# Splitting h's combinations in the up turns, and preparing the weights of down's first two turns together

## The chip, the core and the metric

The kernel runs on one core of a Trainium2 chip. Its time is the device time in microseconds; the kernel before has a median of 2336.82 us over 3 runs (2336.71 to 2340.5). The engines are PE (TensorE, the matmuls), DVE (VectorE), ACT (ScalarE), POOL (GpSimd, which also issues some transfers) and SP (SyncE, which only issues transfers).

## The reference

One layer of a streaming encoder: a combined input projection, a pooling mixer and a differential attention side by side, an output projection, a SwiGLU feed-forward and a final norm. All is float32. The change lies in the feed-forward alone:

```python
def _swiglu(h, g_ffn, w_gate, w_up, w_down):
    n = _rmsnorm(h, g_ffn)
    return h + (jax.nn.silu(n @ w_gate) * (n @ w_up)) @ w_down
```

D_MODEL is 2048 and D_FF 5632. 576 tokens (16 meta, 512 prompt, 64 sample) go through it together.

## The kernel before

**Arithmetic.** Each large product is made by Strassen and Winograd's scheme: a 2x2 block product with seven block products instead of eight, on combinations of the operands' blocks. Every operand is split in a high part (rounded to fp32r by an ACT copy) and a low part (operand minus high, on DVE), and a block product is the sum of high·high, high·low and low·high, three matmuls (L804 to L806) of 128x128 by 128x288. The class `Seven` makes one such turn: `load` fetches four raw weight blocks (L783, on SP), `prep(i)` makes the combinations (L789 to L793, DVE) and their split (L833/L834 in gate/up, L1030/L1031 in down: ACT then DVE), `product(i)` issues the matmuls of product i into one of three PSUM banks and calls the evacuation. Products 3, 4, 5 and 6 reuse the banks of products 0, 1, 2 and 4, so product 6 can start only when the evacuation of product 4 has read its bank. `run` walks over all (turn, product) steps and issues `prep` three products ahead of `product`.

**Stages.** Input projection, attention, output projection, then gate/up from about 850 us to 1776 us, down to about 2300 us, and the final norm with its output.

**Gate/up.** `seq` holds 44 turns: for f = 0 to 21 a gate turn (PSUM banks `mm`) and an up turn (banks `pj`), 168 matmuls each. The evacuations i = 0 to 6 of a turn are made in `inner`: i=0 an ACT copy (L860), i=1 (L862), i=2 (L865, the tile `t5`), i=3 (L867), i=4 (L869), i=5 (L871), i=6 (L873) on DVE. After the last, POOL multiplies by the gate (L875, L876), and in `up_evac` makes four combinations of the seven blocks of h (L904 to L907), in the tile `ho` of 128 x 7 x 288, and stores it to DRAM as `hd[f]` (L908, 1008 KB, issued by POOL). The engines' queues are in order: what stands behind a waiting instruction waits too.

**Down.** 40 turns n, by rounds r and output blocks m. The turns of the first round contract over 2, 2, 3, 3, 4, 4, 5, 5 values of f, later ones over 5. `h_operand` (L1015) loads a piece of `hd[f]` (288 KB for q < 3, 144 KB for q = 3) into a staging tile `sx`, and `h_split` (L952 ACT, L953 DVE) splits it into a slot: 20 full slots (16 of them, `act`, free when gate/up's operands are done) and 7 half slots. The pieces q = 0 to 2 of f = 0 and 1 are loaded (L967) and split already during the last up turn. Evacuations are an ACT copy (L1044) in the first round, later a DVE addition (L1050) or a POOL transfer that accumulates (L1048).

Of the kernel before, what the change touches and what calls it, by code (L numbers as in the profile page):

```python
# [19 lines left out]
P = 128  # L20
# [30 lines left out]
def hymba_step(  # L51
# [717 lines left out]
    class Seven:  # L769


        def __init__(self, src, j0, nj, c0, raws, tmp, splits, xs_, psum, evac):
            self.src = src.rearrange("(j two p) n -> p two j n", p=P, two=2)[:, :, j0:j0 + nj, c0:c0 + 2 * P]
# [75 lines left out]
    hd = [dram.tile([P, 7, TN], F32, name=f"hd{j}") for j in range(FT // 2)]  # L849
# [46 lines left out]
    def up_evac(f):  # L896
        def evac(s, i):
            if i == 0:
                s.ho = fw.tile([P, 7, TN], F32, name="ho")
            h = s.ho  # L900
            inner(s, i, (h[:, 0], h[:, 6], h[:, 3], h[:, 5], h[:, 3:6:2]), blocks(gates[f]))
            if i == 6:
                tt = nc.gpsimd.tensor_tensor
                tt(h[:, 2], h[:, 6], h[:, 0], op=ALU.subtract)  # L904
                tt(h[:, 1], h[:, 5], h[:, 2], op=ALU.subtract)
                tt(h[:, 4], h[:, 5], h[:, 6], op=ALU.subtract)
                tt(h[:, 6], h[:, 3], h[:, 1], op=ALU.subtract)  # L907
                nc.gpsimd.dma_start(out=hd[f], in_=h)  # L908
        return evac
# [30 lines left out]
    FULL, HALF, ACTS = 20, 7, KT  # L940
    hc, nfull, queue = {}, [0], [(f, q) for f in range(NFP) for q in range(4)]

    def full_slot(shape, name, dtype=F32R):
        k = nfull[0]
        nfull[0] += 1
        if k % FULL < ACTS:
            return act.tile(shape, dtype, name=name, tag="act")
        return dw.tile(shape, dtype, name=name, tag="hc", bufs=FULL - ACTS)
# [6 lines left out]
    EARLY = 2  # L955

    def early_operands(n, i):
        if n < len(seq) - 1 or i not in (1, 2, 3):
            return
        if i == 1:  # L960
            for f in range(EARLY):
                for q in range(3):
                    hc[f, q] = full_slot([P, 2, 2, TN], f"hc{q}")
        for f in range(EARLY):
            r = fw.tile([P, 8, P], F32, name="raw", bufs=5)
            s = r.rearrange("p k c -> p (k c)")[:, :2 * TN].rearrange("p (q t) -> p q t", q=2)
            nc.sync.dma_start(out=s, in_=hd[f][:, 2 * i - 2:2 * i])  # L967
            h_split(f, i - 1, s)
# [16 lines left out]
    first_use = {f: min(n for n, (m, f0, f1) in enumerate(turns) if f0 <= f < f1) for f in range(NFP)}  # L985

# [16 lines left out]
    rw.tile([P, 2, TN], F32, name="sx", tag="sx", bufs=3)  # L1003
    yt += [rw.tile([P, 4, TN], F32, name=f"y{m}") for m in range(4, NR)]
    def h_free(f, q, n, i):

        if q == 3:
            return f < HALF or (last_use[f - HALF], 6) <= (n, i)
        k = 3 * f + q - FULL
        return k < 0 or (last_use[k // 3], (1, 4, 5)[k % 3]) <= (n, i)  # L1010

    def h_operand(f, q):
        w = 2 if q < 3 else 1
        s = rw.tile([P, 2, TN], F32, name="sx", tag="sx", bufs=3)
# [86 lines left out]
    seq = []  # L1101
    for n, (m, j0, j1) in enumerate(turns):
        psum = (lambda: banks(pz, "mm", "mm")) if n % 2 == 0 else (lambda: banks(pj, "pj", "pj"))
        seq.append(Seven(w_down[0], j0, j1 - j0, m * 2 * P,
                         lambda n, nj=j1 - j0: rw.tile([P, DJ, P], F32, name="raw", tag="raw", bufs=6)[:, :nj],
                         lambda nj=j1 - j0: rw.tile([P, DJ, P], F32, name="wt", tag="wt", bufs=1)[:, :nj],
                         split_block, lambda i, j, j0=j0: hc[j0 + j, i // 2][:, i % 2], psum, down_evac(n, m)))
    seq[0].load()
    while queue[0][0] < turns[0][2]:
        fq = queue.pop(0)  # L1110
        if fq not in hc:
            h_operand(*fq)
# [4 lines left out]
    run(seq, hooks, order=(1, 0, 2, 4, 3, 5, 6))  # L1117
# [60 lines left out]
```

## Time and profile before

| | us |
|---|---|
| median of 3 runs | 2336.82 |
| span of the profiled execution | 2332.2 |
| PE busy | 2257.0 (97%) |
| DVE busy | 1883.4 (81%) |
| ACT busy | 1149.1 (49%) |
| POOL busy | 507.5 (22%) |

The profiled execution has a span of 2332.2 us, 4.6 us less than the median of the runs. Times within it count from its start. A row of the timeline reads: start, duration, engine, line, operation, output <- input, shapes, count, and in brackets the idle time ahead of it with what ended it. A row of the table by windows reads: window, length, then busy time and number of instructions of PE, PE's weight loads, DVE, ACT and POOL, the granted clock of PE, the busy share of the DMA engines and the rate in GB/s.

### The profile page before, as it was taken

What the parts mean: (1) busy time and instruction counts of PE and PEld (TensorE: products, weight loads), DVE (VectorE), ACT (ScalarE), POOL (GpSimd) and SP (SyncE); (2) the same over time, 40 slices, a digit from 0 to 9 for tenths busy, and PEclk for the clock granted to TensorE, in tenths of its full rate; (3) what the DMA queues carried; (4) which work ended last, traced back from release to release, by engine and by line L of the source; (5) the groups of instructions that cost most, each with busy time, mean ns of one, the idle gap of its engine ahead of it and who ended that gap; (6) DMA issues with size and microseconds to landing.
All of it is one profiled execution on the core that took longest, in us unless ns stands there. A gap on an engine that the chain in (4) does not pass through costs nothing.

```text
span 2332.2 us, 43585 instructions
## 1 busy us (share of the span) xinstructions
PE 2257.0 (97%) x16815; PEld 2231.5 (96%) x16815; DVE 1883.4 (81%) x3474; ACT 1149.1 (49%) x2423; POOL 507.5 (22%) x461
## 2 busy tenths in 40 slices
PE   7999999999999899999999999999997999999995
PEld 6999999999999899999999999999997999999994
DVE  6888888875477888888888888888887778888887
ACT  5666666643244544444444444444445555555544
POOL 1100000001225132322322323323231012211222
PEclk9999999999999999999999999999999999999998
DMA  6433333223234333433434333343344479867643
GB/s 174 113 89 102 90 97 106 72 73 93 79 88 123 106 114 109 136 109 118 125 111 122 115 126 118 110 134 117 104 138 150 135 185 202 207 168 179 162 96 112
DMA packets 426370, 286.00 MB, mean 123 GB/s; under 512 B 13075, under 2 KB 405453, under 8 KB 426164
## 3 DMA queue, kind: packets, MB, share of 16 engines
q1 hardware_dynamic: 403184, 226.50, 33.8%
q0 software_dynamic: 22144, 55.30, 9.6%
q8 instruction: 132, 2.16, 0.4%
q10 hardware_dynamic: 836, 1.43, 0.2%
q14 instruction: 74, 0.61, 0.1%
HBM read 233.65 MB, written 40.35 MB: 117 GB/s over the span
## 4 chain that ended last, share of the span: by engine, by line
PE 88%; DVE 4%; issue 3%; DMA 3%; ACT 1%; POOL 0%; SPq 0%; DVEq 0%; ACTq 0%; POOLq 0%
PE pj L804 10%; PE pj L806 10%; PE mm L804 10%; PE pj L805 10%; PE mm L806 10%; PE mm L805 10%; PE pj L112 6%; PE pj L114 6%; PE pj L113 6%; PE mm L113 3%; PE mm L112 3%; PE mm L114 3%; DMA sx<-hd 1%; DVE ws L1031 1%; PE S L426 1%
## 5 line engine op out<-in xcount | busy, mean ns | idle before, releaser
L834 DVE TENSOR_TENSOR ws<-raw,ws 128x512 fp32r<-128x512 f32 x430 | 384.1, 909 | 74.1 <-ACT ws L833 71.6
L833 ACT ACTIVATE ws<-raw 128x512 fp32r<-128x512 f32 x430 | 264.6, 630 | 345.7 <-PE pj L806 122.2
L804 PE MATMUL mm<-xc,ws 128*128 128x288 f32 x1232 | 365.3, 297 | 7.7 <-ACT ws L833 7.5
L804 PE MATMUL pj<-xc,ws 128*128 128x288 f32 x1232 | 365.1, 296 | 3.1 <-ACT ws L833 3.1
L805 PE MATMUL mm<-xc,ws 128*128 128x288 f32 x1232 | 363.4, 295 | 0.0
L805 PE MATMUL pj<-xc,ws 128*128 128x288 f32 x1232 | 363.2, 295 | 0.0
L806 PE MATMUL pj<-xc,ws 128*128 128x288 f32 x1232 | 361.7, 294 | 0.8 <-DVE ws L834 0.8
L806 PE MATMUL mm<-xc,ws 128*128 128x288 f32 x1232 | 361.6, 293 | 0.2 <-DVE ws L834 0.2
L112 PE MATMUL pj<-x,ws 128*128 128x296 f32 (+1 forms) x1024 | 317.9, 311 | 9.1 <-ACT x L106 8.5
L113 PE MATMUL pj<-x,ws 128*128 128x296 f32 (+1 forms) x1024 | 306.8, 300 | 0.0
L114 PE MATMUL pj<-x,ws 128*128 128x296 f32 (+1 forms) x1024 | 305.3, 298 | 0.0
L804 PEld LDWEIGHTS mm<-xc,ws 128*128 128x128 f32 x1232 | 231.8, 188 | 8.5 <-ACT ws L833 8.0
L804 PEld LDWEIGHTS pj<-xc,ws 128*128 128x128 f32 x1232 | 232.0, 188 | 3.3 <-ACT ws L833 3.3
L806 PEld LDWEIGHTS pj<-xc,ws 128*128 128x128 f32 x1232 | 233.2, 189 | 1.1 <-DVE ws L834 1.1
L806 PEld LDWEIGHTS mm<-xc,ws 128*128 128x128 f32 x1232 | 233.2, 189 | 0.4 <-DVE ws L834 0.4
L805 PEld LDWEIGHTS mm<-xc,ws 128*128 128x128 f32 x1232 | 232.9, 189 | 0.1
L805 PEld LDWEIGHTS pj<-xc,ws 128*128 128x128 f32 x1232 | 232.9, 189 | 0.0
L137 ACT ACTIVATE ws<-wraw,vcols 128x128 fp32r<-128x128 f32 x512 | 169.5, 392 | 106.8 <-PE pj L114 87.7
L112 PEld LDWEIGHTS pj<-x,ws 128*128 128x128 f32 x1024 | 193.1, 189 | 14.3 <-ACT x L106 9.2
L1030 ACT ACTIVATE ws<-raw 128x640 fp32r<-128x640 f32 (+3 forms) x200 | 133.5, 673 | 130.3 <-DVE raw L791 44.4
L113 PEld LDWEIGHTS pj<-x,ws 128*128 128x128 f32 x1024 | 193.7, 189 | 0.4
L114 PEld LDWEIGHTS pj<-x,ws 128*128 128x128 f32 x1024 | 192.8, 188 | 0.0
(338 smaller groups left out, 5772.0 us busy)
## 6 DMA issues: line engine op xcount, KB each, us to landing
raw<-in_w_up_dram SPq DMA_DIRECT2D x88, 512.0 KB, 3.8
raw<-in_w_gate_dram SPq DMA_DIRECT2D x84, 512.0 KB, 3.8
raw<-in_w_down_dram SPq DMA_DIRECT2D x112, 320.0 KB, 4.4
wraw<-in_w_in_dram SPq DMA_DIRECT2D x64, 512.0 KB, 4.1
hd<-ho POOLq DMA_DIRECT2D x22, 1008.0 KB, 5.7
sx<-hd SPq DMA_DIRECT2D x60, 288.0 KB, 3.7
wraw<-in_w_out_dram SPq DMA_DIRECT2D x32, 512.0 KB, 3.9
y<-ev POOLq DMA_DIRECT2D x60, 144.0 KB, 3.7
```

Source lines behind the costliest of these rows:

```text
L112: nc.tensor.matmul(ps, lhsT=w(0), rhs=x(0), start=first, stop=False)
L113: nc.tensor.matmul(ps, lhsT=w(0), rhs=x(1), start=False, stop=False)
L114: return nc.tensor.matmul(ps, lhsT=w(1), rhs=x(0), start=False, stop=last)
L137: nc.scalar.activation(ws[:, 0, k, :], r[:, k, :], AF.Copy, scale=g)
L426: nc.tensor.matmul(ps, lhsT=self.q[:, 2 + m, qs], rhs=kt[:, m, c0:c1], start=False, stop=True)
L804: nc.tensor.matmul(ps, lhsT=w(0), rhs=x(0), start=first and j == 0, stop=False, skip_group_check=True)
L805: nc.tensor.matmul(ps, lhsT=w(0), rhs=x(1), start=False, stop=False, skip_group_check=True)
L806: mm = nc.tensor.matmul(ps, lhsT=w(1), rhs=x(0), start=False, stop=j == self.nj - 1, skip_group_check=True)
L833: nc.scalar.activation(ws[:, 0], src[:, k:k + WK], AF.Copy)
L834: nc.vector.tensor_tensor(ws[:, 1], src[:, k:k + WK], ws.bitcast(F32)[:, 0], op=ALU.subtract)
L1030: nc.scalar.activation(ws[:, 0], src, AF.Copy)
L1031: nc.vector.tensor_tensor(ws[:, 1], src, ws.bitcast(F32)[:, 0], op=ALU.subtract)
```

## The change

**Storing.** For f < 21, `up_evac` splits the seven blocks of h on the spot. ACT copies blocks 0 to 3 to a tile `hi` in fp32r (128x1152), DVE subtracts it from them in place, POOL stores `hi`; the same for blocks 4 to 6 (128x864); then POOL stores the low parts. `hi` has the tag `xlast`, of which there is one buffer. `hd[f]` gets a further axis of two, high and low. f = 21 is stored unsplit.

**Loading.** `h_operand` loads high and low straight into the slot, 576 KB (q < 3) or 288 KB, with no staging tile and no split. For f = 21 the piece comes block by block through `ev` tiles and is split as before. The slots are 16 `act` and 5 `hc`, given out by when they come free; the half slots are 5 and 3.

**Weights of down's turns 0 and 1.** A `Seven` with two output blocks at once loads, combines and splits them during the last up turn into seven `we` tiles in act slots. The first 14 products of down alternate between the two turns. The rest of down goes as before, with turn 2's raw weights loaded ahead of the loop, and h pieces of f >= 3 issued behind them.

```diff
-    hd = [dram.tile([P, 7, TN], F32, name=f"hd{j}") for j in range(FT // 2)]
+    hd = [dram.tile([P, 7, 2 if j < FT // 2 - 1 else 1, TN], F32, name=f"hd{j}") for j in range(FT // 2)]
...
                 tt(h[:, 6], h[:, 3], h[:, 1], op=ALU.subtract)
-                nc.gpsimd.dma_start(out=hd[f], in_=h)
+                if f == FT // 2 - 1:
+                    nc.gpsimd.dma_start(out=hd[f][:, :, 0], in_=h)
+                    return
+                for q, w in ((0, 4), (4, 3)):
+                    hi = fs.tile([P, 4, TN], F32R, name="hi", tag="xlast")
+                    nc.scalar.activation(hi[:, :w], h[:, q:q + w], AF.Copy)
+                    nc.vector.tensor_tensor(h[:, q:q + w], h[:, q:q + w], hi.bitcast(F32)[:, :w], op=ALU.subtract)
+                    nc.gpsimd.dma_start(out=hd[f][:, q:q + w, 0], in_=hi.bitcast(F32)[:, :w])
+                nc.gpsimd.dma_start(out=hd[f][:, :, 1], in_=h)
...
-    def h_split(f, q, s):
-        t, w = hc[f, q], 2 if q < 3 else 1
-        nc.scalar.activation(t[:, 0:w, 0], s[:, :w], AF.Copy)
-        nc.vector.tensor_tensor(t[:, 0:w, 1], s[:, :w], t.bitcast(F32)[:, 0:w, 0], op=ALU.subtract)
...
+    def h_operand(f, q):
+        w, t = 2 if q < 3 else 1, h_slot(f, q)
+        if f < NFP - 1:
+            nc.sync.dma_start(out=t.bitcast(F32), in_=hd[f][:, 2 * q:2 * q + w])
+            return
+        for i in range(w):
+            s = dw.tile([P, TN], F32, name="ev", tag="ev", bufs=4)
+            nc.sync.dma_start(out=s, in_=hd[f][:, 2 * q + i, 0])
+            nc.scalar.activation(t[:, i, 0], s, AF.Copy)
+            nc.vector.tensor_tensor(t[:, i, 1], s, t.bitcast(F32)[:, i, 0], op=ALU.subtract)
...
+    def split_early(src):
+        step = ORDER.index((0, 1, 2, 4, 3, 5, 6)[len(early.w)])
+        n = EARLY * turns[0][2]
+        t = full_slot([P, 1152], "we", (EARLY - 1, step))[:, :2 * n * P].rearrange("p (i j c) -> p i j c", i=2, j=n)
+        nc.scalar.activation(t[:, 0], src, AF.Copy)
+        nc.vector.tensor_tensor(t[:, 1], src, t.bitcast(F32)[:, 0], op=ALU.subtract)
+        return t
...
+        if i == 3:
+            early.load()
+        if i in (0, 1, 3):
+            for f in range(2):
+                h_operand(f, (0, 1, None, 2)[i])
+        for p in ((), (), (), (0, 1), (2, 4), (3, 5, 6), ())[i]:
+            early.prep(p)
...
         if queue and h_free(*queue[0], n, i):
-            h_operand(*queue.pop(0))
+            later = n < EARLY and queue[0][0] >= 3
+            with tc.issue_after(down[EARLY].loaded.ins) if later else ExitStack():
+                h_operand(*queue.pop(0))
...
+        if n < EARLY:
+            down[n].w = {i: lambda k, j, t=t, n=n: t[:, k, 2 * n + j, :] for i, t in early.w.items()}
...
-    run(seq, hooks, order=(1, 0, 2, 4, 3, 5, 6))
+    run(down, hooks, done=7 * EARLY, order=ORDER)
```

The numbers of lines move by 3 to 5 around this place: L833/L834 become L837/L838, the evacuations L860 to L873 become L864 to L877 (i=4 is L873 now), POOL's L904 to L907 become L908 to L911; the new lines are L917 (ACT copy to `hi`), L918 (DVE subtraction), L919 (POOL stores of `hi`), L920 (store of the low parts), L988 (h loads) and L1002/L1003 (split of the early weights).

How the instructions stand in DVE's queue during a gate turn, from behind L873 of the up turn that precedes it; before (`g` is the gate turn's result, `ws` and `wt` are weights):

```order
L834 TENSOR_TENSOR ws<-raw,ws 128x512 x4
L862 TENSOR_TENSOR pu<-mm,pu 128x288
L834 TENSOR_TENSOR ws<-wt,ws 128x512 x2
L789 TENSOR_TENSOR wt<-raw 128x1024
L865 TENSOR_TENSOR t_14935<-mm,pu 128x288
L834 TENSOR_TENSOR ws<-raw,ws 128x512
L790 TENSOR_TENSOR raw<-raw 128x1024
L834 TENSOR_TENSOR ws<-raw,ws 128x512
L867 TENSOR_TENSOR g<-mm,rp 128x288
L834 TENSOR_TENSOR ws<-raw,ws 128x512 x2
L791 TENSOR_TENSOR raw<-wt,raw 128x1024
L869 TENSOR_TENSOR g<-mm,t_14935 128x288
```

With the change, from the evacuation i=1 on (two splits, the first L918 of 128x1152 and two more splits stand between L877 and it):

```order
L866 TENSOR_TENSOR pu<-mm,pu 128x288
L838 TENSOR_TENSOR ws<-wt,ws 128x512
L918 TENSOR_TENSOR ho<-ho,hi 128x864
L838 TENSOR_TENSOR ws<-wt,ws 128x512
L869 TENSOR_TENSOR t_15015<-mm,pu 128x288
L793 TENSOR_TENSOR wt<-raw 128x1024
L838 TENSOR_TENSOR ws<-raw,ws 128x512 x2
L794 TENSOR_TENSOR raw<-raw 128x1024
L871 TENSOR_TENSOR g<-mm,rp 128x288
L838 TENSOR_TENSOR ws<-raw,ws 128x512 x2
L795 TENSOR_TENSOR raw<-wt,raw 128x1024
L873 TENSOR_TENSOR g<-mm,t_15015 128x288
```

The second subtraction L918 stands ahead of the evacuations i=2 to i=4 of the gate turn (L869, L871, L873).

ACT's queue at the same place, with the change; before, the rows are the same without the two L917:

```order
L837 ACTIVATE ws<-raw 128x512 x2
L917 ACTIVATE hi<-ho 128x1152
L864 ACTIVATE pu<-mm 128x288
L837 ACTIVATE ws<-raw 128x512 x2
L837 ACTIVATE ws<-wt 128x512
L917 ACTIVATE hi<-ho 128x864
L837 ACTIVATE ws<-wt 128x512
L837 ACTIVATE ws<-raw 128x512 x6
L837 ACTIVATE ws<-wt 128x512 x2
```

And POOL's, one up turn's end:

```order
L879 TENSOR_TENSOR ho<-ho,g 128x288
L908 TENSOR_TENSOR ho<-ho 128x288
L880 TENSOR_TENSOR ho<-ho,g 128x2x288
L909 TENSOR_TENSOR ho<-ho 128x288
L910 TENSOR_TENSOR ho<-ho 128x288
L911 TENSOR_TENSOR ho<-ho 128x288
L919 DMA hd_9867<-hi 128x4x288
L919 DMA hd_9867<-hi 128x3x288
L920 DMA hd_9867<-ho 896x1x288
```

The second `hi` of ACT uses the buffer that the first L919 reads; the three stores take the place of one.

SP's queue where down's turn 3 gets its raw weights (128x3x128, the second group of four); f is `hd_9862` plus its number; `sx` is the staging tile. Before:

```order
L1015 DMA sx<-hd_9864 128x576 x3
L783 DMA raw<-in_w_down_dram 128x2x128 x2
L1015 DMA sx<-hd_9864 128x288
L783 DMA raw<-in_w_down_dram 128x3x128
L1015 DMA sx<-hd_9865 128x576 x2
L783 DMA raw<-in_w_down_dram 128x3x128
L1015 DMA sx<-hd_9865 128x576
L1015 DMA sx<-hd_9865 128x288
L1015 DMA sx<-hd_9866 128x576
L783 DMA raw<-in_w_down_dram 128x3x128
L1015 DMA sx<-hd_9866 128x576
L783 DMA raw<-in_w_down_dram 128x3x128
```

With the change:

```order
L988 DMA hh<-hd_9869 128x576
L786 DMA raw<-in_w_down_dram 128x3x128 x4
L988 DMA hc_20901<-hd_9865 128x1152
L988 DMA hc_20910<-hd_9865 128x1152
L988 DMA hc_20919<-hd_9865 128x1152
L988 DMA hh<-hd_9865 128x576
L988 DMA hc_20940<-hd_9866 128x1152
L988 DMA hc_20949<-hd_9866 128x1152
L988 DMA hc_20958<-hd_9866 128x1152
L988 DMA hh<-hd_9866 128x576
L988 DMA hc_20986<-hd_9867 128x1152
L786 DMA raw<-in_w_down_dram 128x3x128 x4
```

Before, the raw weights of turns 2 and 3 alternate with loads of h. Now turn 2's four come together, and nine loads of h (f = 3, 4 and the first of 5) follow, the last one ahead of turn 3's four.

More of the change, by code (lines that the diff above doesn't have):

```diff
@@ L769, in hymba_step, with __init__ @@
     class Seven:
[L772 to L773 removed]
+        def __init__(self, src, j0, nj, c0, raws, tmp, splits, xs_, psum, evac, turns=1):
+            self.src = src.rearrange("(j two p) n -> p two j n", p=P, two=2)[:, :, j0:j0 + nj, c0:c0 + 2 * turns * P]
+            self.turns = turns
             self.nj, self.raws, self.tmp, self.splits, self.xs_, self.psum, self.evac = nj, raws, tmp, splits, xs_, psum, evac
@@ L781, in load @@
             for n, two, c in (("11", 0, 0), ("21", 0, 1), ("22", 1, 1), ("12", 1, 0)):
-                self.a[n] = t = self.raws(n)
-                nc.sync.dma_start(out=t, in_=self.src[:, two, :, c * P:c * P + P])
+                self.a[n] = a = self.raws(n)
+                for t in range(self.turns):
+                    b0 = (2 * t + c) * P
+                    self.loaded = nc.sync.dma_start(out=a[:, t * self.nj:t * self.nj + self.nj],
+                                                    in_=self.src[:, two, :, b0:b0 + P])
         def prep(self, i):
@@ L939, in hymba_step @@
     DJ, NFP, NR = 5, FT // 2, KT // 2
[L940 to L948, printed above, removed]
-    def h_split(f, q, s):
-        t, w = hc[f, q], 2 if q < 3 else 1
-        nc.scalar.activation(t[:, 0:w, 0], s[:, :w], AF.Copy)
-        nc.vector.tensor_tensor(t[:, 0:w, 1], s[:, :w], t.bitcast(F32)[:, 0:w, 0], op=ALU.subtract)
[L955 to L968, printed above, removed]
-    run(seq, early_operands, begin=3, done=5)
-    ffb.close()
-    ffa.close()
-    ffr.close()
-    wts_stack.close()
+    ORDER = (1, 0, 2, 4, 3, 5, 6)
     starts = (2, 2, 3, 3, 4, 4, 5, 5)
@@ L985, in hymba_step, with slot_free, full_slot @@
     first_use = {f: min(n for n, (m, f0, f1) in enumerate(turns) if f0 <= f < f1) for f in range(NFP)}
+    ACTS, HCS, HALF = KT, 5, (5, 3)
+    END = (NR * 5, 0)
+    hc, queue = {}, [(f, q) for f in range(NFP) for q in range(4)]
+    now, taken = [(0, -1)], {"act": [(0, -1)] * ACTS, "hc": [END] * HCS}
+    def slot_free():
+        return min(min(t) for t in taken.values()) <= now[0]
+    def full_slot(shape, name, until=END, dtype=F32R):
+        tag = min(taken, key=lambda t: min(taken[t]))
+        assert min(taken[tag]) <= now[0]
+        taken[tag].remove(min(taken[tag]))
+        taken[tag].append(until)
+        if tag == "act":
+            return act.tile(shape, dtype, name=name, tag="act")
+        return dw.tile(shape, dtype, name=name, tag="hc", bufs=HCS)
@@ new lines, in hymba_step @@
+    EARLY = 2
+    def split_early(src):
[5 more added lines that the diff above has]
+        return t
+    early = Seven(w_down[0], 0, 2, 0, lambda n: fw.tile([P, 8, P], F32, name="raw", bufs=5)[:, :4],
+                  lambda: fw.tile([P, 8, P], F32, name="wt")[:, :4], split_early, None, None, None, turns=EARLY)
@@ L987, in hymba_step, with early_operands @@
+    def early_operands(n, i):
+        if n < len(seq) - 1:
+            return
+        if i == 3:
[5 more added lines that the diff above has]
+            early.prep(p)
+    run(seq, early_operands, begin=3, done=5)
+    ffb.close()
+    ffa.close()
+    ffr.close()
+    wts_stack.close()
     dw = ctx.enter_context(tc.tile_pool(name="dw", bufs=1, reuse_waits="tile"))
@@ L1099, in finished @@
             rows_out(turns[n - 1][0])
-    seq = []
+    down = []
     for n, (m, j0, j1) in enumerate(turns):
         psum = (lambda: banks(pz, "mm", "mm")) if n % 2 == 0 else (lambda: banks(pj, "pj", "pj"))
[L1104 to L1112, printed above, removed]
+        down.append(Seven(w_down[0], j0, j1 - j0, m * 2 * P,
+                          lambda n, nj=j1 - j0: rw.tile([P, DJ, P], F32, name="raw", tag="raw", bufs=6)[:, :nj],
+                          lambda nj=j1 - j0: rw.tile([P, DJ, P], F32, name="wt", tag="wt", bufs=1)[:, :nj],
+                          split_block, lambda i, j, j0=j0: hc[j0 + j, i // 2][:, i % 2], psum, down_evac(n, m)))
+        if n < EARLY:
+            down[n].w = {i: lambda k, j, t=t, n=n: t[:, k, 2 * n + j, :] for i, t in early.w.items()}
+            down[n].a = {}
+    for f in range(2):
+        h_operand(f, 3)
+    down[EARLY].load()
     def hrow(m):
         return yt[m // 2].rearrange("p (i c) t -> p i (c t)", i=2)[:, m % 2]
-    run(seq, hooks, order=(1, 0, 2, 4, 3, 5, 6))
+    run(down, hooks, done=7 * EARLY, order=ORDER)
     rows_out(NR - 1)
```

39 lines of the change are left out of this document (21 added, 18 removed).

## The prediction

> **What bounds the kernel now.** I read the page's busy times first, then the work per stretch, then the waits of TensorE, then single rows. The page:
>
> ```profile
> span 2332.2 us, 43585 instructions
> PE 2257.0 (97%) x16815; PEld 2231.5 (96%) x16815; DVE 1883.4 (81%) x3474; ACT 1149.1 (49%) x2423; POOL 507.5 (22%) x461
> ```
>
> Busy time by stretches (columns: PE, weight loads, DVE, ACT, POOL, granted clock, DMA share, GB/s): one gate/up pair f, the seam from gate/up into down, then down.
>
> ```profile
> 1421.60:1465.90 44.30, 44.30 (x339) 44.30 (x338) 38.03 (x49) 19.04 (x31) 13.13 (x10) 1.00 0.39 119
> 1780.00:1800.00 20.00, 13.89 (x76) 12.65 (x77) 13.78 (x31) 12.28 (x32) 1.55 (x3) 0.83 0.67 206
> 1800.00:1820.00 20.00, 13.28 (x80) 12.58 (x79) 16.28 (x31) 12.77 (x28) 0.00 (x0) 0.83 0.76 223
> 1820.00:1850.00 30.00, 29.72 (x224) 29.33 (x223) 23.48 (x40) 18.16 (x37) 0.00 (x0) 1.00 0.44 129
> 1880.00:1950.00 70.00, 69.11 (x515) 68.32 (x514) 54.24 (x84) 34.21 (x58) 15.53 (x18) 1.00 0.85 198
> 1950.00:2020.00 70.00, 70.00 (x527) 69.83 (x526) 59.63 (x92) 38.43 (x66) 16.41 (x19) 1.00 0.93 216
> ```
>
> A gate/up pair keeps PE busy without a hole, with DVE at 38 of 44.3 us: the pair can only lose. Down from 1820 is PE-bound too, with its DMA queues at 0.85 to 0.93. Only the seam has something to win. Its rows on PE, the last matmul of up and the first of down's turns 0, 2, 3 and 4:
>
> ```profile
> 1775.87 0.29 PE L806 MATMUL pj<-xc,ws 128*128 128x288 f32 x1
> ...
> 1780.95 0.61 PE L804 MATMUL mm<-hc,ws 128*128 128x288 f32 x1 [4.79 <-ACT ws L1030]
> ...
> 1806.60 0.61 PE L804 MATMUL mm<-hc,ws 128*128 128x288 f32 x1 [3.31 <-ACT ws L1030]
> ...
> 1819.21 0.40 PE L804 MATMUL pj<-hc,ws 128*128 128x288 f32 x1 [1.73 <-ACT ws L1030]
> ...
> 1828.08 0.40 PE L804 MATMUL mm<-hc,ws 128*128 128x288 f32 x1 [0.28 <-ACT ws L1030]
> ```
>
> A gate turn has 168 matmuls in 22.16 us, from its first matmul to the first of the up turn:
>
> ```profile
> 1421.44 0.29 PE L804 MATMUL mm<-xc,ws 128*128 128x288 f32 x1
> ...
> 1443.60 0.29 PE L804 MATMUL pj<-xc,ws 128*128 128x288 f32 x1
> ```
>
> That is 0.132 us each, so down's turns 0 to 3 (42+42+63+63 = 210) are worth 27.7 us. They take from 1776.0 to 1828.08, 52.1 us. The seam loses 24.4 us; PE waits, and some of its matmuls run at half the clock after the longer holes:
>
> ```profile
> 1782.00:1784.00 2.00, 2.00 (x9) 2.00 (x10) 1.88 (x6) 1.13 (x3) 0.00 (x0) 0.50 0.81 165
> 1806.00:1810.00 4.00, 3.40 (x14) 3.40 (x15) 3.04 (x6) 2.83 (x6) 0.00 (x0) 0.50 0.60 188
> ```
>
> **The seam: what is removed.** The weights of turns 0 and 1 are combined and split during the last up turn, in act slots that the interleaved turns 0 and 1 read. The work is 7 ACT copies, 7 DVE splits and 4 combinations of 128x512 (11 × 0.60 = 6.6 us of DVE, by the spacing below); up's last turn has half of the pair's 44.3 − 38.0 us of DVE free, some 3,, but there it no longer splits h, nor prepares turns 0 and 1 in pieces of 128x256. So turns 0 and 1 should start at once and end 11.1 us after 1776.0. Turn 2 then waits on DVE, whose queue puts the y additions of turn 1 (L1050, now L1090) ahead of turn 2's combinations (now L793 to L795); turn 3 waits on SP's queue, where nine h loads, seven of 576 KB and two of 288, now stand between the raw weights of turns 2 and 3. Those nine are 4.7 MB, 21 to 23 us at the 223 to 206 GB/s of the seam's rows, so turn 3 should start some 23 us after 1776.0, where 19.4 would be the full rate. I put holes of 1.7, 2.6 and 2.5 us ahead of turns 2, 3 and 4, 6.8 in all, each between none and the 3.31 seen before. Gain 24.4 − 6.8 = **−17.6 us**; ends: −24.4 with no hole, −14.5 with three of 3.3.
>
> **Gate/up: what is added, 21 times.** After POOL's h combinations ACT copies h[0:4] into `hi` (128x1152), DVE subtracts, POOL stores; then the same for h[4:7] (128x864). There is one `hi` buffer, so the second copy waits until the first copy's store has *landed*, and the second subtraction stands in DVE's queue behind that, ahead of the evacuations of the next gate turn. Product 6 of that gate turn writes the PSUM bank of product 4, so it waits for the evacuation i=4 (L869 before, L873 after). Rows of one pair before, DVE:
>
> ```profile
> 1422.80 0.45 DVE L873 TENSOR_TENSOR ho<-pj,pu 128x288 f32<-128x288 f32 x1
> 1423.17 3.74 DVE L834 TENSOR_TENSOR ws<-raw,ws 128x512 fp32r<-128x512 f32 x3
> ...
> 1432.50 0.68 DVE L834 TENSOR_TENSOR ws<-raw,ws 128x512 fp32r<-128x512 f32 x1
> 1433.10 1.22 DVE L790 TENSOR_TENSOR raw<-raw 128x1024 f32<-128x1024 f32 x1
> 1434.23 0.68 DVE L834 TENSOR_TENSOR ws<-raw,ws 128x512 fp32r<-128x512 f32 x1
> 1434.84 0.45 DVE L867 TENSOR_TENSOR g<-mm,rp 128x288 f32<-128x288 f32 x1
> 1435.20 0.68 DVE L834 TENSOR_TENSOR ws<-raw,ws 128x512 fp32r<-128x512 f32 x1
> ...
> 1438.41 0.45 DVE L869 TENSOR_TENSOR g<-mm,t 128x288 f32<-128x288 f32 x1
> ```
>
> L869 ends at 1438.86. Product 6 is the last seventh before 1443.60, so it starts at 1440.43: 1.57 us of slack. Spacings when DVE runs back to back: 0.60 for 128x512 (1432.50 to 1433.10), 1.13 for 128x1024, 0.36 for 128x288; between them 0.96 for 128x864 and 1.27 for 128x1152.
>
> POOL's rows, the ACT group of the same size as the new copy, and the landing times that bracket the new store:
>
> ```profile
> 1423.33 1.81 POOL L876 TENSOR_TENSOR ho<-ho,g 128x576 f32<-128x576 f32 x1 [2.26 <-DVE ho L873]
> 1425.22 1.14 POOL L905 TENSOR_TENSOR ho<-ho 128x288 f32<-128x288 f32 x1
> ...
> 1427.65 1.14 POOL L907 TENSOR_TENSOR ho<-ho 128x288 f32<-128x288 f32 x1
> 1429.09 0.59 POOL L908 DMA_DIRECT2D hd<-ho  x1 [0.30 <-POOL ho L907]
> ```
>
> ```profile
> L875 POOL TENSOR_TENSOR g<-g,rp 128x288 f32<-128x288 f32 x22 | 17.9, 813 | 267.0 <-DVE g L871 267.0
> L892 ACT ACTIVATE g<-g 128x1152 f32<-128x1152 f32 x22 | 25.8, 1171 | 28.1 <-POOL g L876 28.1
> ```
>
> ```profile
> hd<-ho POOLq DMA_DIRECT2D x22, 1008.0 KB, 5.7
> ...
> hres<-hp POOLq DMA_DIRECT2D x8, 576.0 KB, 3.9
> ...
> out_dram<-stg POOLq DMA_DIRECT2D x16, 256.0 KB, 2.8
> ```
>
> Step by step in the pair's own times: DVE does two splits after 1423.17 and is then held by the first subtraction, so POOL runs its last three combinations almost alone, at the 0.81 of L875 and not 1.14, from 1425.2 to about 1427.8. The first copy starts after the second of its four inputs' combinations, 1426.2, and ends at 1427.4. Store issued 1428.1 (0.30 after POOL is free); landed 3.9 later, 1432.0. Second copy 0.92, to 1432.95. DVE by then has done the first subtraction and what stands behind it, and has idled since about 1431.4. From 1433.0 it must do: subtraction 0.96, five splits 3.0, two evacuations 0.72, three combinations 3.4, and L873 0.45, 8.5 us: 1441.5. Product 6 wanted it at 1440.43. PE waits about 1.1 us in every pair, **21 × 1.15 = +24 us** (the 1.15 with the queue step between ACT and DVE). DVE has 6 us free per pair less 2.25 for the new subtractions, so the delay does not pile up; it recurs.
>
> Ends: a landing of 2.8 us (the 256 KB row) leaves no stall, 0; 5.7 us (the 1008 KB row) gives 1.15 + 1.8 = 2.95 each, +62. The new store has 576 KB, the size of the hres row, hence 3.9. The weights themselves aren't late: they are split several products ahead. The other two stores per pair add bytes at a DMA share of 0.39, and nobody waits for them.
>
> The Trainium skill, page "DMA: Bandwidth & Descriptors", section on the anatomy of one DMA on the gpsimd path, gives about 2.0 us plus bytes over 436e3 per us for a POOL-issued transfer, most of the fixed part being the write receipt. For 589,824 bytes that estimate is 3.35 us, and it would make the stall 0.6 us and the term +13; the hres row says 3.9, and I go by the row.
>
> **Down.** ACT and DVE lose the h splits, which is worth nothing since PE sets the time there. Loads of h double: between 1880 and 2020 the h loads were 19 of 288 KB and 7 of 144 KB, 6.5 MB, and as much again goes on 29 MB:
>
> ```profile
> DMA packets 35362, 29.00 MB, mean 207 GB/s; under 512 B 1648, under 2 KB 31856, under 8 KB 35349
> ...
> sx<-hd SPq DMA_DIRECT2D x19, 288.0 KB, 4.4
> ...
> sx<-hd SPq DMA_DIRECT2D x7, 144.0 KB, 5.2
> ```
>
> At 0.85 to 0.93 this fills the engines: 35.5 MB at the best seam rate of 223 GB/s take 159 us, 19 more than the stretch. Much can move to 1820 to 1880 and past 2020, where shares are lower, as far as slots are free. I take +4, ends 0 and +14. The last f, split on arrival by small pieces through `ev`, adds 1 at most 3.
>
> **Sum.** −17.6 + 24 + 4 + 1 = +11.4 on the span of 2332.2, so 2343.6. The median lies 4.6 above the profiled span (2336.8 against 2332.2): **2348 us**.
>
> **The rivals.**
> 1. *The landing is hidden* (faster side). If the first store lands within 2.8 us of issue, or DVE's work behind the subtraction goes faster, nothing is late: −17.6 + 5 = −12.6, 2324. For it: without the landing DVE would reach L873 at 1431.4 + 8.5 = 1439.9, ahead of 1440.43. Against it: 3.9 in the hres row. The sign turns where the stall is 0.6 us (17.6 − 5 over 21), a landing of 3.35.
> 2. *Almost even*: stalls of 0.4 to 0.8, landing 3.2 to 3.5, gives −4 to +4, about 2337. The estimate from the Trainium skill's page above would end here.
> 3. *The stall is 2 us and more*: POOL's combinations keep their 1.14 (store issued 1 us later, 1429.1) or the store shares the engines with up's raw loads and lands like hd, 5.7. Then +42 to +62 − 12.6: 2366 to 2386. The 1008 KB row speaks for it, the free DMA share against.
> 4. *The seam keeps its loss*, because DMA binds it: the doubled h loads move the holes from turns 0 and 1 to turns 3 to 5. With a gain of 8 instead of 17.6 and the stall as forecast, 2357.
>
> **How the numbers follow.** A measurement of this kernel tells 0.2%, 4.7 us, from no change. Forecast (2342 to 2356) 0.36; rival 1 0.29; rival 2 0.17; rival 3 0.09; rival 4 0.09. Faster: rival 1 and a little of 2, 0.33. Same: the rest of 2 and the forecast's lower edge, 0.18. Slower: 0.49. Range 2321 to 2368, which holds rivals 1, 2, 4 and the start of 3; the forecast's own range is 2338 to 2358.
>
> **What would show it.** In the profile after: PE idle in gate/up named as waiting for DVE L873, about 1 us, 21 times, and none before product 6; the second copy L917 released by the first store of L919, and DVE idle ahead of the second L918; the first L919 landing in 3.9 us. At the seam: turn 0 right behind the last up matmul, turn 4 some 34.5 us later, clock near 1.00. In down: PE idle below 5 us between 1880 and 2280 of before's work. The prediction is wrong if gate/up keeps its 44.3 us per pair, or if turn 4 starts less than 14 us earlier than before relative to the last up matmul.

## The result and the profile after

The changed kernel takes 2378.41 us (median of 4 runs, 2376.1 to 2379.22), the kernel before 2336.77 us beside it: a ratio of 1.0172, 95% interval 1.0155 to 1.0188. It is slower, as forecast, but by 42 us and not by 11, and outside the range that ended at 2368.

The head of the page of the changed kernel:

```profile
span 2377.4 us, 43444 instructions
PE 2272.0 (96%) x16815; PEld 2242.4 (94%) x16815; DVE 1851.6 (78%) x3424; ACT 1128.5 (47%) x2377; POOL 541.2 (23%) x503
```

DVE and ACT have less to do than before and the time is longer: what was taken off lay under cover, what was added lies on the path. PE's rows with the change mark the three stretches; first matmul of the gate turn f = 1 (in the kernel before it starts at 845.28), last of the last up turn and first of down, and the first matmuls of down's turns 2, 3 and 4:

```profile
845.18 0.29 PE L808 MATMUL mm<-xc,ws 128*128 128x288 f32 x1
...
1818.46 0.29 PE L810 MATMUL pj<-xc,ws 128*128 128x288 f32 x1
1818.59 0.29 PE L808 MATMUL mm<-hc,we 128*128 128x288 f32 x1
...
1834.89 0.61 PE L808 MATMUL mm<-hc,ws 128*128 128x288 f32 x1 [4.83 <-ACT ws L1070]
...
1849.03 0.61 PE L808 MATMUL pj<-hc,ws 128*128 128x288 f32 x1 [3.78 <-ACT ws L1070]
...
1861.74 0.40 PE L808 MATMUL mm<-hc,ws 128*128 128x288 f32 x1 [2.52 <-ACT ws L1070]
```

| stretch | before | with the change | difference | forecast |
|---|---|---|---|---|
| gate/up, 42 turns from f = 1 | 930.7 | 973.4 | +42.7 | +24 |
| seam, end of up to turn 4 | 52.1 | 43.2 | −8.9 | −17.6 |
| from turn 4 to the end | 504.1 | 515.7 | +11.6 | +5 |

The differences add up to the 45.2 us between the spans (ahead of f = 1 the changed kernel is 0.1 us shorter). Each span is that of one execution; the medians are 41.6 us apart. All three terms came out worse than forecast.

**Gate/up.** The change adds its work to 21 pairs of a gate and an up turn. The waits of PE between 1050 and 1800, which hold 16 of them, are one line (there was none between 1050 and 1740 before; engine, line, waited for, us in total, times, longest):

```profile
PE mm L808 <- DVE g L873: 24.4, 16, 3.1
```

It is the wait that was forecast. One pair of it, DVE first, then ACT, POOL, and PE's product 6:

```profile
1448.93 0.45 DVE L877 TENSOR_TENSOR ho<-pj,pu 128x288 f32<-128x288 f32 x1
...
1454.18 1.36 DVE L918 TENSOR_TENSOR ho<-ho,hi 128x1152 f32<-128x1152 f32 x1 [2.36 <-POOL ho L911]
...
1458.71 1.06 DVE L918 TENSOR_TENSOR ho<-ho,hi 128x864 f32<-128x864 f32 x1 [1.00 <-ACT hi L917]
...
1466.95 0.45 DVE L873 TENSOR_TENSOR g<-mm,t 128x288 f32<-128x288 f32 x1
```

```profile
1452.53 1.17 ACT L917 ACTIVATE hi<-ho 128x1152 fp32r<-128x1152 f32 x1 [2.85 <-POOL ho L909]
...
1457.75 0.93 ACT L917 ACTIVATE hi<-ho 128x864 fp32r<-128x864 f32 x1 [2.20 <-DVE ws L838]
```

```profile
1454.09 0.83 POOL L919 DMA_DIRECT2D hd<-hi  x1
```

```profile
1467.55 0.37 PE L808 MATMUL mm<-xc,ws 128*128 128x288 f32 x1 [1.18 <-DVE g L873]
```

The first store is issued at 1454.09 and the second copy starts at 1457.75, 3.66 us later (the bracket names another releaser, which had been done before; the program makes the copy wait for that store). The median landing of these stores is 3.6:

```profile
hd<-hi POOLq DMA_DIRECT2D x16, 576.0 KB, 3.6
```

From the start of the second copy to L873's end there are 9.65 us, where the forecast had 9.4 (0.92 for the copy, 8.5 for DVE), and PE waits 1.18 us, where it had 1.15. Twelve of the 21 pairs look like this one, two have 0.8, and seven have more, from 1.34 to 3.14. The hole follows the landing of the first store: landings of 3.58, 3.96, 4.71, 5.06 and 5.53 us go with holes of 1.18, 1.57, 2.32, 2.67 and 3.14, the landing less 2.39 each time.

What the forecast left out is what a hole costs beside its length. A pair with a hole of 1.18 us is 1.47 longer than before, so restarting costs 0.29. And after the longest holes the clock drops. In one pair the first store took 5.5 us to land and PE waited 3.14 us. These are rows of the DMA view between this store's issue and its landing (of a queue: number, kind, packets, MB, share of the 16 engines), then those of the usual pair above:

```profile
q8 instruction: 1, 0.02, 1.0%
...
hd<-hi POOLq DMA_DIRECT2D x1, 576.0 KB, 5.5
```

```profile
q0 software_dynamic: 144, 0.59, 45.9%
q1 hardware_dynamic: 497, 0.25, 23.2%
...
hd<-hi POOLq DMA_DIRECT2D x1, 576.0 KB, 3.6
```

The slow one has a packet of a queue of the kind `instruction` beside it. So has each of the nine pairs whose first store landed after more than 3.65 us; the 12 that landed after 3.56 to 3.63 us have none. No run takes these packets away, so that they cause the late landings is not shown.

The stretch behind the hole of 3.14 us, then that of a pair with a hole of 2.32 us:

```profile
1511.50:1515.20 3.70, 0.64 (x5) 0.40 (x3) 3.60 (x6) 0.32 (x1) 0.00 (x0) 0.91 0.81 230
1515.20:1521.20 6.00, 5.92 (x25) 5.95 (x26) 4.17 (x6) 1.98 (x4) 1.16 (x1) 0.50 0.00 0
```

```profile
1234.00:1236.00 2.00, 1.24 (x5) 1.27 (x6) 1.59 (x4) 1.64 (x3) 0.00 (x0) 0.66 0.44 130
1236.00:1238.00 2.00, 2.00 (x10) 2.00 (x9) 1.29 (x3) 0.03 (x1) 1.17 (x1) 0.50 0.00 0
```

Half the clock for some 6 us costs about 3 us, so that pair is 6.0 longer for a hole of 3.1. In all: 21 × 1.18 = 24.8 for the usual hole, 6 for the late landings, 21 × 0.29 = 6 for restarts, and the remaining 6 for half clock make the 42.7.

**The seam and down.** The transfers of the first 11 us behind up, and of the 32 us to turn 4, then a stretch around turn 16, where the one long hole of down is:

```profile
1819.00:1830.00 11.00, 11.00 (x83) 10.74 (x81) 2.18 (x5) 3.58 (x10) 4.76 (x6) 1.00 0.99 338
1830.00:1862.00 32.00, 20.88 (x129) 20.27 (x129) 15.89 (x31) 11.62 (x27) 0.00 (x0) 0.84 0.92 324
...
2020.00:2048.00 28.00, 24.55 (x166) 24.34 (x165) 17.45 (x26) 9.45 (x15) 4.32 (x5) 0.88 1.04 290
```

The DMA engines are full in both places (0.92 to 1.04). PE starts down at once and does turns 0 and 1 without a hole, as forecast; then the raw weights of turn 2 are late: issued from 1822.47 on, while h loads fill the engines, they hold DVE up for 2.3 us,

```profile
1832.30 0.56 DVE L793 TENSOR_TENSOR wt<-raw 128x384 f32<-128x384 f32 x1 [2.31 <-DMA raw<-in_w_down_dram]
```

and the holes ahead of turns 2, 3 and 4 are 4.83, 3.78 and 2.52, 11.1 us in all, where 1.7, 2.6 and 2.5 were forecast. With 27.7 us of matmuls at full rate that makes 38.8 of the 43.2 us; the other 4.4 are restarts and half clock behind the holes (0.84 in the second row). In turn 16 DVE waits 6.1 us for raw weights behind a burst of h loads, and an evacuation stands behind that wait in its queue:

```profile
DVE wt L793 <- DMA raw<-in_w_down_dram: 6.1, 1, 6.1
```

PE stands still for 3.4 us there and runs at half clock after it; that turn alone costs 6.2 of the 11.6 us, and another 1.4 lie in turn 4, behind its hole of 2.52.

### The profile page after: what moved, and what is told of

Its sections match the earlier page's. It is cut to its first block, busy times and chain, and to the rows that moved or that the text cites. A ratio compares the mean times of both kernels' runs of the same rounds, so it can differ in the third digit from the quotient of the medians.

```text
span 2377.4 us, 43444 instructions
## 1 busy us (share of the span) xinstructions
PE 2272.0 (96%) x16815; PEld 2242.4 (94%) x16815; DVE 1851.6 (78%) x3424; ACT 1128.5 (47%) x2377; POOL 541.2 (23%) x503
## 4 chain that ended last, share of the span: by engine, by line
PE 67%; DVE 15%; DMA 5%; issue 5%; POOL 4%; ACT 3%; SPq 0%; ACTq 0%; DVEq 0%; POOLq 0%
PE pj L810 9%; PE pj L808 9%; PE pj L809 9%; PE pj L112 6%; PE pj L114 5%; PE pj L113 5%; DVE ws L838 5%; PE mm L808 4%; PE mm L810 4%; PE mm L809 4%; PE mm L114 3%; PE mm L112 3%; PE mm L113 3%; DMA hd<-hi 2%; DMA raw<-in_w_down_dram 2%
## 5 line engine op out<-in xcount | busy, mean ns | idle before, releaser
L837 ACT ACTIVATE ws<-raw 128x512 fp32r<-128x512 f32 x430 | 256.8, 627 | 340.1 <-DVE raw L795 145.1
L838 DVE TENSOR_TENSOR ws<-raw,ws 128x512 fp32r<-128x512 f32 x430 | 367.5, 890 | 50.5 <-ACT ws L837 50.1
L808 PE MATMUL mm<-xc,ws 128*128 128x288 f32 x1232 | 369.5, 300 | 38.5 <-DVE g L873 31.1
L808 PEld LDWEIGHTS mm<-xc,ws 128*128 128x128 f32 x1232 | 234.3, 190 | 43.6 <-issue 35.7
L810 PEld LDWEIGHTS mm<-xc,ws 128*128 128x128 f32 x1232 | 235.4, 191 | 0.4 <-DVE ws L838 0.4
L809 PEld LDWEIGHTS mm<-xc,ws 128*128 128x128 f32 x1232 | 235.3, 191 | 0.1
L1070 ACT ACTIVATE ws<-raw 128x640 fp32r<-128x640 f32 (+3 forms) x190 | 130.0, 687 | 147.0 <-DVE raw L795 52.1
```

What stands on the lines that cost most here:

```text
L808: nc.tensor.matmul(ps, lhsT=w(0), rhs=x(0), start=first and j == 0, stop=False, skip_group_check=True)
L809: nc.tensor.matmul(ps, lhsT=w(0), rhs=x(1), start=False, stop=False, skip_group_check=True)
L810: mm = nc.tensor.matmul(ps, lhsT=w(1), rhs=x(0), start=False, stop=j == self.nj - 1, skip_group_check=True)
L837: nc.scalar.activation(ws[:, 0], src[:, k:k + WK], AF.Copy)
L838: nc.vector.tensor_tensor(ws[:, 1], src[:, k:k + WK], ws.bitcast(F32)[:, 0], op=ALU.subtract)
L1070: nc.scalar.activation(ws[:, 0], src, AF.Copy)
```

## The experiments

Two theories of gate/up's loss were tried first. Theory A: the second copy's wait for the landing makes it. Theory B: the added DVE work does, wherever the copy stands. For the seam and down there are three: the doubled bytes of h, the order of SP's queue, or the work on DVE. The two halves of the change were also tried alone. Times are compared by their ratio to the kernel before, which ran beside each.

### A second buffer

```diff
-                    hi = fs.tile([P, 4, TN], F32R, name="hi", tag="xlast")
+                    hi = fs.tile([P, 4, TN], F32R, name="hi", tag="xlast") if q == 0 else \
+                        fw.tile([P, 4, TN], F32R, name="hi", tag="g")
```

> The change, but the second high part (blocks 4 to 6) goes into the gate tile's buffer, which is free by then, so its copy no longer waits for the first store to land; the work stays the same. Theory A (the wait for the landing makes the stall): a gate/up pair takes 44.3 us again, PE waits for L873 below 2 us in all, the 42.6 us that gate/up lost come back, 2336 us (2333 to 2340). Theory B (the 2.25 us of added DVE work ahead of the evacuation i=4 make the stall, wherever the copy stands): the stall of about 1 us per pair stays, 2360 us or more.

Measured: 2346.68 us, 1.0036 (1.002 to 1.0052). Gate/up takes 941.75 us, 31.7 of the 42.7 us came back. PE's wait between 1050 and 1780:

```profile
PE mm L808 <- DVE g L873: 3.6, 16, 0.2
```

0.23 us per pair instead of 1.5, and no pair has more than 0.3. So A holds for three quarters: with the wait go the half clock and what the late landings cost (three of these stores still took 4.5 to 5.0 us to land). B holds for the rest: 0.53 us per pair stay, 0.23 of waiting and 0.3 of restart. Seam (43.6) and down are as in the change. The time is above the 2340 that A alone allowed and below the 2360 that B alone asked for.

### One subtraction less

```diff
                     nc.scalar.activation(hi[:, :w], h[:, q:q + w], AF.Copy)
-                    nc.vector.tensor_tensor(h[:, q:q + w], h[:, q:q + w], hi.bitcast(F32)[:, :w], op=ALU.subtract)
+                    if q == 0:
+                        nc.vector.tensor_tensor(h[:, q:q + w], h[:, q:q + w], hi.bitcast(F32)[:, :w], op=ALU.subtract)
```

> The kernel with the second buffer without its second subtraction (the low parts of blocks 4 to 6 are left out: h itself is stored in their place, so the output differs). DVE does 0.97 us less ahead of the evacuation i=4 in each pair. If DVE's added work is what still costs 0.53 us per pair there (0.23 us of waiting and the restart), gate/up falls by 11 us and the time is 2336 us (2333 to 2338). If the residue comes from elsewhere (the copies on ACT, the stores), it stays at 2346.

Measured: 2336.39 us, 0.9992 (0.9983 to 1.0002). Gate/up takes 931.2 us against 930.7 before the change, and PE has no wait in it. So the residue lies in DVE's chain ahead of L873, which is too long by 0.2 us, and that little costs 11 us, since each pair pays the restart. Both theories are needed. Taking 0.97 us of work out of the chain ends the wait, but it is not the only slack there: in this kernel too DVE stands idle for 2.35 us ahead of its first subtraction, waiting for POOL's last combination. Whether a shorter wait there would do as well wasn't tried.

### The two halves alone

Early weights only; h is stored unsplit and split after loading, with the slots of before:

```diff
-                if f == FT // 2 - 1:
-                    nc.gpsimd.dma_start(out=hd[f][:, :, 0], in_=h)
-                    return
...
+                nc.gpsimd.dma_start(out=hd[f][:, :, 0], in_=h)
...
+            s = staging[0].tile([P, 2, TN], F32, name="sx", tag="sx", bufs=3)
+        nc.sync.dma_start(out=s[:, :w], in_=hd[f][:, 2 * q:2 * q + w, 0])
+        nc.scalar.activation(t[:, 0:w, 0], s[:, :w], AF.Copy)
+        nc.vector.tensor_tensor(t[:, 0:w, 1], s[:, :w], t.bitcast(F32)[:, 0:w, 0], op=ALU.subtract)
```

> Only the second half of the change: early weights of down's turns 0 and 1 as in the change, but h stored unsplit and split after loading, as before. Theory A with the doubled h loads as what ate the seam's gain: gate/up 44.3 us per pair, down as before, the four turns of the seam in about 40 us instead of 52 (43 with the change): 2325 us (2318 to 2330). Rival: the seam's remaining holes are DVE's and SP's order and not bytes, and the h splits come back on top, so the seam takes 44 to 50 us: 2329 to 2335.

Measured: 2341.29 us, 1.0006 (0.9992 to 1.002), a miss for both. Gate/up is 930.72 us, to the hundredth that of before, so early weights cost nothing there. But the seam takes 50.3 us, only 1.8 less than before. PE's waits in it:

```profile
PE mm L808 <- ACT ws L1065: 6.9, 2, 4.1
PE mm L808 <- ACT we L995: 4.3, 1, 4.3
PE pj L808 <- ACT ws L1065: 3.7, 1, 3.7
```

The early weights themselves are late (L995), and the later turns' weights stand behind h splits. In ACT's queue ahead of turn 2, for instance, a split that waits for its load stands in front of the weights:

```profile
1797.59 0.68 ACT L985 ACTIVATE hc<-sx 128x576 fp32r<-128x576 f32 x1 [1.19 <-DMA sx<-hd]
1798.18 0.51 ACT L1065 ACTIVATE ws<-raw 128x384 fp32r<-128x384 f32 x1
```

What is left of the gain is lost after turn 4: from there to the last matmul it takes 5.3 us longer than before, though h has the bytes and the splits that it had before. Of these, 1.7 lie in turn 4 (half clock behind the hole of 4.1 us ahead of it) and 2.3 in turns 16 and 17.

Split only, without early weights. The order that keeps h loads of f >= 3 behind turn 2's raw weights goes with them:

```diff
-        if i == 3:
-            early.load()
...
-        for p in ((), (), (), (0, 1), (2, 4), (3, 5, 6), ())[i]:
-            early.prep(p)
...
-    run(down, hooks, done=7 * EARLY, order=ORDER)
+    run(down, hooks, order=ORDER)
```

> Only the first half: h split and stored in gate/up and loaded split, but no early weights, down's turns 0 and 1 prepared one after the other as before. If the halves add up, gate/up loses 42.6 us, down 11, and the seam takes about 52 us as before: 2390 us (2383 to 2397). Rival: the missing h splits alone make the seam as short as in the change (43 us), so the early weights were worth nothing: 2378 us.

Measured: 2376.66 us, 1.0161 (1.0129 to 1.0192), the rival's number. The first hole is back,

```profile
1828.26 0.61 PE L808 MATMUL mm<-hc,ws 128*128 128x288 f32 x1 [10.41 <-ACT ws L1064]
```

and the holes ahead of turns 2, 3 and 4 are 1.4, 0.6 and 0.1 instead of 4.8, 3.8 and 2.5: the seam takes 46.2 us, 3 more than with early weights. Gate/up and the way from turn 4 to the last matmul are 1.7 and 1.8 shorter, so nothing of the 3 is left, and the intervals of the two ratios (1.0161 and 1.0172) overlap. My reading is that turns 0 and 1, started earlier, meet the same transfers a little later. In this kernel a hole of 1.90 us in gate/up was followed by half clock,

```profile
1374.93 0.37 PE L808 MATMUL mm<-xc,ws 128*128 128x288 f32 x1 [1.90 <-DVE g L873]
```

```profile
1375.50:1378.00 2.50, 2.50 (x12) 2.50 (x11) 1.96 (x4) 0.89 (x3) 1.05 (x1) 0.50 0.00 0
```

while in the kernel with early weights only the hole of 2.78 us ahead of turn 2 was not.

### The order of SP's queue

On the kernel with the second buffer:

```diff
-        if queue and h_free(*queue[0], n, i):
-            later = n < EARLY and queue[0][0] >= 3
-            with tc.issue_after(down[EARLY].loaded.ins) if later else ExitStack():
-                h_operand(*queue.pop(0))
+        if queue and h_free(*queue[0], n, i) and (n >= EARLY or queue[0][0] < 3):
+            h_operand(*queue.pop(0))
```

> As the kernel with the second buffer, and loads of h for f of 3 and more are issued only from turn 2 on, behind the raw weights of turn 3. If SP's order makes the hole ahead of turn 3 (3.8 us in the change, with half clock behind it), the hole falls below 2 us and the time is 3 us (1 to 6) below that of the kernel with the second buffer. If the bytes of the h loads make it, the hole only moves to turn 4 or 5 and the time is within 1.5 us of it.

Measured: 2339.82 us, 1.0006 (0.9991 to 1.0021), against 1.0036 with the second buffer alone, on the same chip: 6.9 us less, more than the 1 to 6 expected. The seam falls from 43.6 to 37.5 us; the hole ahead of turn 3 is gone (0.00), that ahead of turn 4 falls from 2.48 to 1.53, that ahead of turn 2 stays (5.39, where it was 4.63). For turn 3 it was the order: loads that nobody needed yet stood ahead of those that it waited for.

### Half the bytes of h

On the kernel with the second buffer; each part of h lies together in DRAM, and from f = 5 on the high parts alone are loaded and used twice:

```diff
+            if f >= DJ:
+                nc.sync.dma_start(out=t.bitcast(F32).rearrange("p i k t -> p (i k) t")[:, :w], in_=hd[f][:, 0, 2 * q:2 * q + w])
+                return
```

> The kernel with the second buffer, but from f = 5 on down loads only the high parts of h and uses them in place of the low parts too (the low parts of those f are left out of the product, so the output differs): the h loads of the later rounds have the bytes that they had before the change, all else stays. If the doubled bytes make down's loss, down from turn 4 to its end falls from 492.8 to about 484 us (482.1 before the change) and the time is 8 us (5 to 10) below the kernel with the second buffer, with no hole over 1 us ahead of turn 16's later products. If the slots and the order of SP's queue make it, down stays above 490 us and the time within 2 us.

Measured: 2336.59 us, 0.9999 (0.9989 to 1.0008). Against the second buffer alone that is 0.0037 or 8.6 us less, as expected if the bytes make it. From turn 4 to the end of the matmuls it is 0.8 us shorter than before the change, where the second buffer alone had 10.6 more (2.3 of these in its last turn, which in the whole change, with the same loads, is nearly as short as before). PE's waits from turn 4 on, first with the second buffer, then with half the bytes (some 7 us of it is the tail's, which the kernel before has too):

```profile
PE mm L808 <- DVE y L1091: 7.3, 6, 2.9
PE pj L808 <- DVE y L1091: 3.5, 3, 2.0
PE mm L808 <- ACT ws L1071: 2.5, 1, 2.5
```

```profile
PE mm L808 <- DVE y L1095: 4.2, 4, 2.1
PE pj L808 <- DVE y L1095: 3.7, 3, 2.2
```

The 28 us around turn 16, with half the bytes and then with the second buffer alone:

```profile
1987.50:2015.50 28.00, 26.81 (x200) 26.17 (x199) 19.38 (x29) 11.43 (x20) 6.93 (x8) 1.00 0.95 226
```

```profile
1989.30:2017.30 28.00, 25.14 (x178) 24.94 (x178) 17.95 (x27) 10.42 (x17) 5.17 (x6) 0.94 1.05 290
```

PE is busy 1.7 us longer, and its clock stays at 1.00. So with half the bytes, and no splits in their place, down's loss is gone. (The layout in DRAM differs too; that it doesn't matter wasn't tried by itself.) The bytes are not the whole story of down, though: kernels that load and split the later h as before the change still take longer than before from turn 4 to the last matmul, by 5.3 us (early weights only, above), 6.0, 2.3 and 8.0 (the three of the next section, the second of which has no early weights). What costs them this is open.

### Splitting where the seam reads

h split in gate/up for f = 0 to 4 only, on the kernel with second buffer and SP's new order; later f as before the change, with the staging tile back and one full slot and one half slot fewer:

```diff
+    NSPLIT = 5
-    hd = [dram.tile([P, 7, 2 if j < FT // 2 - 1 else 1, TN], F32, name=f"hd{j}") for j in range(FT // 2)]
+    hd = [dram.tile([P, 7, 2 if j < NSPLIT else 1, TN], F32, name=f"hd{j}") for j in range(FT // 2)]
...
-                if f == FT // 2 - 1:
+                if f >= NSPLIT:
...
+        if f < NSPLIT:
+            nc.sync.dma_start(out=t.bitcast(F32), in_=hd[f][:, 2 * q:2 * q + w])
+            return
+        s = rw.tile([P, 2, TN], F32, name="sx", tag="sx", bufs=3)
```

> Both sides of the change where they pay: h is split in gate/up and loaded split only for f = 0 to 4, which the seam reads; from f = 5 on h is stored and split as before the change. Second buffer, early weights, and h of f of 3 and more behind turn 3's raw weights. If the costs add up as measured: gate/up 5 pairs of 0.53 us = 2.7, seam 37.5 to 39 us instead of 52.1, down 4 to 7 us longer than before: 2331 us (2327 to 2335), faster than before the change. If gate/up's residue or down's loss isn't tied to the later f, 2337 to 2340.

Measured: 2330.4 us, 0.9971 (0.9958 to 0.9984): 0.3% faster than the kernel before, and by the terms as expected: gate/up +2.7, seam 38.1, the rest 6 longer. The same without the early weights:

> The kernel that splits h in gate/up for f = 0 to 4 (2330.4 us, seam 38.1 us), without the early weights: down's turns 0 and 1 load and prepare their weights as before. If the early weights pay where the transfers no longer stand in front of turn 3, the first hole comes back (some 8 to 11 us ahead of turn 0) and the seam is 44 to 49 us, the time 2336 to 2341. If they only move the hole to turn 2, as the pair of the whole change with and without them suggests (seams of 43.2 and 46.2), the time is within 3 us, 2328 to 2334.

Measured: 2333.3 us, 0.997 (0.9953 to 0.9988). The first hole is back at 9.95 us,

```profile
1789.76 0.61 PE L808 MATMUL mm<-hc,ws 128*128 128x288 f32 x1 [9.95 <-ACT ws L1066]
```

and the seam is 43.7 us, but the way from turn 4 to the last matmul is 3.7 us shorter than with them. The first hole and, but for 0.3 us, the seam came as the first expectation had it and the time as the second: early weights shorten the seam by 5.5 us, and the ratios (0.9971 and 0.997) show no gain in time. And with `NSPLIT = 2`:

> The kernel that splits h in gate/up for f = 0 to 4, now for f = 0 and 1 only: f = 2 to 4 come with half the bytes in the seam and are split there by ACT and DVE. If bytes in the seam still set turn 2's hole (raw weights landing 9 us after issue at a DMA share of 1.0), that hole of 4.9 us falls to 3 or less, gate/up's residue falls from 2.7 to 1.1, and the time is 2323 to 2329. If the splits on ACT and DVE are late in their place, the seam is 41 to 45 us and the time 2331 to 2336.

Measured: 2328.62 us, 0.9946 (0.9927 to 0.9966). The time is in the first range. But the hole of 4.9 us that the expectation gave to turn 2 stands ahead of turn 4 in the kernel with five: there the holes ahead of turns 2, 3 and 4 are 2.7, 0.0 and 4.9, here they are 0.9, 3.5 and 4.0. Turn 2's first raw weights are issued 4.3 us ahead of down's first matmul and land 3.2 us later, where with five they were issued 1.1 us behind it and took 9.0. Gate/up has 1.1 us more than before, as expected. The seam is 38.5, no shorter than with five, and the spans of the two profiled executions differ by 1.6 us the other way. Its ratio is the best, but its interval meets that of f = 0 to 4, so which of the two is faster is open.

## Why the prediction was right or wrong

**Gate/up, the step "PE waits about 1.1 us in every pair, 21 × 1.15".** The mechanism and its place were right: L873 is the instruction waited for, and the wait follows the landing. That the usual wait of 1.18 us meets the 1.15 is partly luck: the store landed 0.3 us sooner than the 3.9 taken, and the rest of the chain came out 0.3 us longer. The term was mis-sized at 24 us against 42.7, since it left three things out. A hole of PE costs 0.29 us beyond itself. The landing is not one number: seven of 21 pairs had longer holes, up to the one whose store took 5.5 us. And holes from 2.3 us on here could drop the clock, where the forecast counted no half clock in gate/up. The landing's upper end (5.7, a stall of 2.95) was priced as if it came in all pairs or none; a few pairs with a part of it, and their half clock, cost 12 us. The late landings go with packets of an `instruction` queue; that these make them wasn't tried.

The clause of rival 1 that "without the landing DVE would reach L873 at 1439.9, ahead of 1440.43" was wrong by 0.8 us: with the second buffer L873 was still late by 0.23. The order changed with it (both subtractions stand together, ahead of all the gate turn's evacuations), and the 0.5 us of slack on paper was no margin.

**The seam, the step "I put holes of 1.7, 2.6 and 2.5".** Two things failed, each worth about half of the 8.7 us. The holes came to 11.1 us and not 6.8. And "Gain 24.4 − 6.8" takes the holes off at their bare length, though the prediction's own rows show half clock behind those before: restarts and half clock behind the new ones cost another 4.4 us. Turn 4 came 8.9 us earlier than before, less than the 14 that the prediction had set as a sign of being wrong.

Of turn 2's hole the cause was half right: DVE's queue does hold turn 2's combinations behind y additions, but 2.3 of the 4.83 us are raw weights that came late, at a DMA share of 0.99. Turn 3's wait on SP's order was right, since the hole goes when the h loads stand behind its weights, but its size was not: the rate of 206 to 223 GB/s that it was worked out from was no limit, as the engines moved 338 GB/s, and some 14 MB went through them in the 43 us and not just the 4.7 of the nine loads. And the gain was credited to the early weights; the runs show that the missing h splits gave most of it (52.1 to 46.2 us without early weights), and that early weights alone gave 1.8 us. Rival 4 had this part right, with a gain of 8 and the holes moved to later turns.

**Down, +5.** The doubled bytes as the cause are borne out by the run with half of them, with the open end that kernels with the old bytes there lost 2 to 8 us as well. The size, 11.6, lay within the ends 0 to 14. It too rests on the 223 GB/s, which were passed here (290 around turn 16), and on h loads that are 6.6 MB and not 6.5. What was missing is again that a hole of 3.4 us pays 2.8 more in half clock.

**The sum** was off by 34 us, 18.7 of it in gate/up, 8.7 in the seam, 6.6 in down. Rival 3, "the stall is 2 us and more", gave 2366 to 2386 and has the measured time, but by luck: the stall was 1.5 us on average, 31 us in all where it counted 42 to 62, and the rest of the time came from restarts, half clock and the seam, of which it had the full gain.

Two rules of the Trainium skill can be held against these rows. The page "DMA: Bandwidth & Descriptors", section on the anatomy of one DMA on the gpsimd path, gives 3.35 us for the store of 576 KB as an estimate; the trace has 3.6, between that and the 3.9 taken. The page "TensorE: Matmul & The Clock Gate", section "Why this matters for your kernels", asks for no idle gaps of more than about 3 us; the trace agrees for 3.1 us, but here holes of 1.9, 2.3 and 2.7 us were followed by a clock of 0.50 as well, so the measurement sets the bound lower.

## What to carry to other kernels

Price a wait on the bounding engine with what follows it: here 1.18 us of stall cost 1.47, and 3.1 us cost 6.0. Take a landing as a spread and not as one number: 3.56 to 5.53 us here for one and the same store. Where a buffer comes free by the landing of a store, and what waits for it stands in a queue ahead of evacuations, its wait can become the bounding engine's wait in every turn; a tile that is dead at that moment is a second buffer for nothing. A split that is moved from after a load to before a store doubles the bytes; here the kernels that did so only for what the seam reads were the ones that came out ahead.

## What the runs showed of the hardware

Holes of PE of 2.32 and 2.67 us, and one of 1.90 in the kernel with the split only, were followed by a granted clock of 0.50 for some 3 us; ones of 2.35 and 2.78 were not, and one of 3.14 us was followed by it for some 6. In every trace the clock kept one value for whole multiples of 3.41 us. The DMA engines moved 338 GB/s at a share of 0.99 with h in pieces of 576 and 288 KB, where before the change 223 GB/s went with a share of 0.76. A store of 576 KB issued by POOL landed in 3.56 to 3.63 us in 12 of 21 pairs; in the other nine, with a packet of an `instruction` queue beside it, in 3.68 to 5.53. In the kernel with the split only the four landings over 4.2 us have such a packet too, but ones of 3.98 and 4.13 have none.
